# Strassen products moved from the MLP's up-projection to its down-projection, more low parts made by transfers, one shared transpose for two norms

## The chip, the cores and the metric

The kernel runs on one core of a Trainium2 chip. The core has five engines with a queue of instructions each: PE (TensorE, the matrix unit; its weight loads are shown apart as PEld), DVE (VectorE), ACT (ScalarE), POOL (GpSimd) and SP (SyncE, which here only issues transfers); 16 DMA engines move data between the device's memory and the on-chip SBUF. Matrix products are accumulated in eight PSUM banks. An engine works through its queue in order and waits there for what others have to finish. The metric is the device time of one execution in microseconds (us).

## The reference

The input is one sequence of 512 tokens with 1,024 features, in float32. Layer A attends to keys that a small indexer selects, layer B attends with a forget-gate bias to keys and values computed once from the stream. Each layer ends with the same MLP:

```python
def sq_relu_mlp(xn, w_up, w_down):
    return jnp.square(jax.nn.relu(xn @ w_up)) @ w_down

def reference(...):
    h = x
    for layer in range(DEPTH):
        if layer < N_A:
            h = h + dsa_attention(rms_norm(h, g_attn_a[layer]), w_in_a[layer], w_o_a[layer])
        else:
            if layer == N_A:
                k_sh, v_sh, cum_sh = shared_kv(h, g_kv, w_kv_b, b_f)
            j = layer - N_A
            h = h + fox_attention(rms_norm(h, g_attn_b[j]), w_q_b[j], w_o_b[j], k_sh, v_sh, cum_sh)
        h = h + sq_relu_mlp(rms_norm(h, g_mlp[layer]), w_up[layer], w_down[layer])
    return rms_norm(h, g_final)
```

`w_up` is 1024 x 4096, `w_down` 4096 x 1024. At the start of layer B the stream `h` is normalized twice, with two gains (`g_kv`, `g_attn_b`) and the same root mean square.

## The kernel before

Every float32 product is made of three matmuls (`mm3`): each operand is split into a high part, rounded to the type fp32r, and a low part, the rest; high x high, high x low and low x high are summed in a PSUM bank. The high part is a copy on ACT. The low part comes in one of two ways (`wunit`): a subtraction on DVE, or, where `lo_eng` is POOL, ACT writes the negated high part and a transfer issued by POOL adds the raw weights onto it (tile pair `arena_r<-arena` in the trace, 512 KB each). Before, 20 weight blocks of layer A's attention take the second way; all other blocks take the first.

The MLP (`mlp`) works in four quarters of 1,024 hidden features each. In a quarter the up-projection makes the hidden features, transposed (features on partitions, 512 tokens along the row), ReLU and square follow, and the down-projection (`tokprod`) adds 512 output columns at a time onto the stream `h`: per quarter 192 matmuls of 128x512, named `tp`. In the up-projection, `pair` takes two blocks of 128 features and computes them by Winograd's form of Strassen's scheme: the weights (2 x 2 blocks: inner half by feature block) and the tokens (inner half by token half) are added and subtracted on DVE, seven products instead of eight are made (`prod`, 12 matmuls of 128x256 each, named `st`), and DVE adds the results together. The first four feature blocks of a layer are made plainly (`up`). The weight sums are formed anew for each pair, the token sums (`tokside`) once per layer.

The engines' orders are not those of the code. `Recorder` records all operations; `schedule` then simulates them with its own costs, gives each a due time that follows PE's order, and lets each engine take the ready operation that is due first and finds a buffer; `emit` writes the result out. What it assumes for a matmul, for a transfer and for buffers so decides who stands in front of whom. Buffers are cut from two arenas in SBUF, one for float32 (54 KB a partition) and one for fp32r (144 KB), in any size.

At the end of layer A's MLP, `afterA` is called for each block of 128 tokens: root mean square, product with the gain `g_attn_b`, eight transposes on PE (`yT`), splitting; the same is then repeated with `g_kv` for the keys and values of layer B: 64 transposes in all for the two norms.

## Time and profile before

| | |
|---|---|
| time, median of 3 runs | 1193.82 us (1193.72 to 1194.06) |
| profiled execution: own time | 1194.9 us |
| profiled execution: span in the trace | 1193.1 us |
| PE busy | 1171.7 us, 98% |
| DVE busy | 867.2 us, 73% |
| ACT busy | 656.5 us, 55% |
| POOL busy | 166.0 us, 14% |
| moved by DMA | 126.14 MB, mean 106 GB/s |

Busy time is the union of an engine's instructions, so 98% says that PE has hardly a gap, not that each matmul runs at its best. All operations are emitted from one source line (L454), so that groups are told apart by the names of their tiles: `tp`, `st`, `up`, `qp`, `kp`, `lg`, `pv` and so on are PSUM banks.

### The profile page before, as it was taken

Reading aid. Unit: us, or ns where it says so; the run is one execution under the profiler, and the core shown is the slowest. Engines: PE = TensorE matmul, PEld = TensorE weight load, DVE = VectorE, ACT = ScalarE, POOL = GpSimd, SP = SyncE. Lnnn points to the kernel's source line nnn. Section 1 sums busy time; section 2 is a strip of 40 time slices with the busy share of each in tenths; the row PEclk is TensorE's granted clock in tenths of the full one; section 3 lists DMA queues with packets and bytes.
Section 4 is the critical chain, followed back from the end, with each engine's and each line's share of the span. In section 5 each row is a group of like instructions: output and inputs, shape, how many; then the busy total and the mean of one; then the engine's idle time right before and its main releaser. Section 6 shows DMA issues by size and latency. Waiting matters only on the chain.

```text
span 1193.1 us, 18921 instructions
## 1 busy us (share of the span) xinstructions
PE 1171.7 (98%) x6932; PEld 1027.7 (86%) x6932; DVE 867.2 (73%) x1774; ACT 656.5 (55%) x1309; POOL 166.0 (14%) x303
## 2 busy tenths in 40 slices
PE   8999899999999999999999999999999999999997
PEld 7878677899899899898897888778998998998986
DVE  6799978778486576676766559987785874866753
ACT  7831789748345355364434069985583453452632
POOL 0401444100000000000000077772000000000010
PEclk8999899999999999999999999999999999999999
DMA  9920065616224224425440202543152242242301
GB/s 326 205 54 1 3 192 141 177 39 189 78 68 154 77 70 124 124 69 163 158 126 18 72 24 79 179 127 107 36 181 85 74 139 89 72 141 72 124 2 71
DMA packets 95519, 126.14 MB, mean 106 GB/s; under 512 B 6193, under 2 KB 61489, under 8 KB 95426
## 3 DMA queue, kind: packets, MB, share of 16 engines
q1 hardware_dynamic: 92546, 114.45, 30.1%
q0 software_dynamic: 2880, 10.49, 4.6%
q8 instruction: 55, 0.90, 0.3%
q14 instruction: 38, 0.31, 0.1%
HBM read 110.20 MB, written 4.23 MB: 96 GB/s over the span
## 4 chain that ended last, share of the span: by engine, by line
PE 91%; DVE 3%; ACT 2%; DMA 2%; issue 1%; POOL 0%; SPq 0%; DVEq 0%; POOLq 0%; ACTq 0%
PE tp L454 46%; PE st L454 23%; PE up L454 4%; PE qp L454 4%; PE pv L454 3%; PE lg L454 3%; PE kp L454 3%; PE pT L454 3%; ACT arena_r L454 1%; DVE arena_r L454 1%; PE yT L454 1%; DVE arena L454 1%; ACT arena L454 1%; DMA arena<-in_w_in_a_dram 1%; DMA arena_r<-arena 1%
## 5 line engine op out<-in xcount | busy, mean ns | idle before, releaser
L454 PE MATMUL tp<-arena_r 128*128 128x512 f32 (+3 forms) x2592 | 596.1, 385 | 2.4 <-DMA arena_r<-arena 1.5
L454 PEld LDWEIGHTS tp<-arena_r 128*128 128x128 f32 x2592 | 473.0, 189 | 93.0 <-DMA arena_r<-arena 1.8
L454 DVE TENSOR_TENSOR arena_r<-arena,arena_r 128x512 fp32r<-128x512 f32 (+4 forms) x396 | 321.9, 835 | 153.4 <-PE tp L454 90.1
L454 ACT CAST arena_r<-arena 128x512 fp32r<-128x512 f32 (+5 forms) x416 | 299.5, 752 | 242.8 <-PE tp L454 150.3
L454 PEld LDWEIGHTS st<-arena_r 128*128 128x128 f32 x2352 | 283.4, 192 | 0.6
L454 PE MATMUL st<-arena_r 128*128 128x256 f32 x2352 | 283.8, 283 | 0.0
L454 ACT ACTIVATE arena<-arena 128x512 f32<-128x512 f32 (+1 forms) x162 | 100.6, 627 | 84.3 <-DVE arena L454 77.1
L454 POOL TENSOR_SCALAR arena<-arena,cq 128x128 f32<-128x128 f32 (+3 forms) x64 | 36.4, 583 | 484.7 <-ACT cq L454 475.9
L454 DVE TENSOR_TENSOR arena<-arena 128x512 f32<-128x512 f32 (+4 forms) x145 | 99.3, 699 | 2.6 <-ACT arena L454 1.3
L454 DVE TENSOR_TENSOR arena<-tp,arena 128x512 f32<-128x512 f32 (+1 forms) x81 | 54.9, 683 | 51.0 <-PE tp L454 49.7
L454 DVE TENSOR_TENSOR arena<-st,arena 128x256 f32<-128x256 f32 x196 | 77.0, 418 | 17.5 <-PE st L454 13.8
L454 POOL TENSOR_SCALAR arena<-arena,rc 128x128 f32<-128x128 f32 (+3 forms) x128 | 75.6, 610 | 65.6 <-DVE rc L454 63.2
L454 ACT ACTIVATE arena<-arena,mn 128x384 f32<-128x384 f32 (+3 forms) x128 | 71.4, 562 | 21.6 <-issue 18.1
L454 POOL TENSOR_TENSOR arena<-arena 128x512 f32<-128x512 f32 (+2 forms) x18 | 20.4, 1149 | 411.0 <-DVE arena L454 410.7
L454 DVE CUSTOM_DVE_ANT_0 arena<-lg,arena 128x128 f32<-128x128 f32 (+3 forms) x128 | 58.8, 484 | 10.0 <-PE pT L454 3.1
L454 PE MATMUL lg<-arena_r 128*128 128x128 f32 (+3 forms) x256 | 64.2, 348 | 0.1
L454 PE MATMUL kp<-arena_r 128*128 128x512 f32 x192 | 54.5, 402 | 1.2 <-DVE arena_r L454 1.2
L454 PE MATMUL pT<-ident,arena 128*128 128x128 f32 x320 | 53.2, 281 | 1.8 <-DVE arena_r L454 0.9
L454 PEld LDWEIGHTS pT<-ident,arena 128*128 128x128 f32 x320 | 39.6, 143 | 12.8 <-POOL arena L454 4.7
L454 PEld LDWEIGHTS lg<-arena_r 128*128 128x128 f32 x256 | 43.7, 199 | 6.0 <-issue 1.5
L454 PE MATMUL up<-arena_r 128*128 128x256 f32 x384 | 47.5, 284 | 0.0
L454 PE MATMUL qp<-arena_r 128*128 128x256 f32 (+1 forms) x288 | 47.0, 321 | 0.0
(91 smaller groups left out, 913.6 us busy)
## 6 DMA issues: line engine op xcount, KB each, us to landing
arena<-in_w_up_dram SPq DMA_DIRECT2D x64, 512.0 KB, 4.0
arena<-in_w_down_dram SPq DMA_DIRECT2D x64, 512.0 KB, 3.6
arena_r<-arena POOLq DMA_DIRECT2D x20, 512.0 KB, 6.8
arena<-in_w_kv_b_dram SPq DMA_DIRECT2D x16, 512.0 KB, 4.8
arena<-in_w_in_a_dram SPq DMA_DIRECT2D x12, 512.0 KB, 6.3
arena<-in_x_dram SPq DMA_DIRECT2D x8, 512.0 KB, 6.2
arena<-in_w_o_a_dram SPq DMA_DIRECT2D x8, 512.0 KB, 6.1
arena<-in_w_q_b_dram SPq DMA_DIRECT2D x8, 512.0 KB, 5.1
```

The source lines that it names most:

```text
L454: getattr(self.engs[o.eng], o.fn)(*a, **k)
```

## The change

- The up-projection is computed plainly: per feature block 24 matmuls of 128x512 (for the first four blocks of a layer 48 of 128x256, as before).
- The down-projection takes Strassen's scheme in Winograd's form: 2 x 2 blocks of the hidden activations (token half by half of the quarter's features, tile `sq`) and of the weights (half of the features by half of the output columns). Per quarter there are seven products of 24 matmuls of 128x512 (`tp<-dhi,xhi`). Sums of the weights are made on DVE in place (`raw<-raw`), those of the activations too; results go to `h` and, for the part that two quadrants share, to two tiles `share`. Two pairs of banks are used twice: the second product is accumulated onto the first after DVE (or ACT, in the first quarter) has read the first. Two of the four weight quarters are loaded twice, so that 96 blocks of 512 KB of `w_down` are loaded instead of 64.
- Low parts by transfers ("dl") now also for the up-projections, layer B's queries, values and output projection: 108 blocks instead of 20. Those of the down-projection and of layer B's keys stay on DVE.
- The schedule's costs: 13.3 ns on top of each matmul's columns instead of 3, later landings for POOL's transfers; new limits ("ahead") on how early a weight buffer may be taken. Buffers are now slots of fixed size: 41 of 4 KB, 18 of 2 KB, 7 of 1 KB, 8 of 512 bytes, one of 256 bytes.
- Layer B's two norms share one scaled row tile and 32 transposes; the two gains are applied per feature while the result is split. The gains are loaded as columns of eight values per partition.
- In the last norm the halves change roles for the last token blocks, since the left half of the columns is now the last to be finished.

```diff
+                c = (2.0 if o.eng != "POOL" else 5.0) + o.cost if o.fn == "dma_start" else o.cost + self.LAT.get((o.eng, s.eng), 0.1)
...
+                        if x[2].seq - low >= t.pool.reach or x[2].prio - pec > t.pool.ahead:
...
+    "ahead": {"wr": 40, "wh": 30, "wl": 30},
+    "slots": {1024: 41, 512: 18, 256: 7, 128: 8, 64: 1}, "sizes": (8, 8, 8, 8), "sq": 'S', "x8": 400, "h": 200, "wr": 1500,
...
+    def lows(stage):
+        lo_eng[0] = G if stage in CFG["dl"] else V
...
-        def pair(c0, done):
-            raw = [rec.tile(p_wr, [128, 4, 256], F32, "raw") for _ in range(2)]
...
-            a11 = wop(A[0, 0])
-            a12 = wop(A[0, 1])
...
-            o4 = wop(wsum(A[0, 1], s2, OP.subtract))
-            o3 = wop(wsum(A[0, 0], A[1, 0], OP.subtract))
-            a22 = wop(A[1, 1])
...
-            S.copy(k1, prod(a11, B[0, 0]))
-            add(r1[:, lo], prod(a12, B[1, 0]), k1)
-            add(u2, prod(o2, tm["t2"]), k1)
-            add(z, prod(o1, tm["t1"]), u2)
-            add(r1[:, hi], prod(o4, B[1, 1]), z)
-            S.activation(r1, r1, AF.Relu)
...
-            for f in range(f, nf, 2):
-                pair(f0 + 128 * f, lambda i, r, f=f: relu_done(f + i, r))
...
-            tokprod(hl, wd, f0, nf, 0, 512, addto(0), order="t" if lastc else "k")
...
+        lows("up1" if last else "up0")
...
+        share = [htile([128, 512], "share") for _ in range(2)]
+        def xop(src):
+            out = []
+            for k in range(0, 4, 2):
+                hl = tuple(rec.tile(p_x8, [128, 2, H], F32R, n) for n in ("xhi", "xlo"))
+                split(hl[0], hl[1], src[:, k:k + 2, :])
+                out.append(hl)
+            return out
         def wop(src):
+            out = []
+            for y in src:
+                hl = rec.tile(p_wh, [128, 2, 512], F32R, "dhi"), rec.tile(p_wl, [128, 2, 512], F32R, "dlo")
+                split(hl[0], hl[1], y)
+                out.append(hl)
+            return out
...
+        def part(b, x, w, start, i, c=slice(0, 512), js=range(2)):
+            for j in js:
+                for k in (2 * j, 2 * j + 1):
+                    mm3(b[:, c], tuple(u[:, k % 2, 128 * i:128 * i + 128] for u in x[j]),
+                        tuple(u[:, k % 2, c] for u in w[j]), start and k == 0, k == 3, skip_group_check=True)
+        def prod(bs, x, w, start, whole=False):
+            if whole:
+                for i in range(2):
+                    part(bs[i], x, w, start, i)
+            else:
+                for j in range(2):
+                    for i in range(2):
+                        part(bs[i], x, w, start, i, js=(j,))
...
+            X = {(i, j): rec.tile(p_x8, [128, 4, H], F32, "sq") for i in range(2) for j in range(2)}
+            f0 = 1024 * ci
+            def relu_done(f, b):
+                r = scr([128, T], "r")
+                S.activation(r, b, AF.Relu)
+                for i in range(2):
+                    S.activation(X[i, f // 4][:, f % 4, :], r[:, tl[i]], AF.Square)
...
+            for f in range(f, 8):
+                b = bank([128, T], "up")
+                featprod(xT, wS(wu, f0 + 128 * f), b)
+                relu_done(f, b)
+            def raw(j, n):
+                ys = []
+                for k in range(f0 + 512 * j, f0 + 512 * j + 512, 256):
+                    ys.append(rec.tile(p_wr, [128, 2, 512], F32, "raw"))
+                    SP.dma_start(ys[-1], wd[k:k + 256, 512 * n:512 * n + 512].rearrange("(k p) c -> p k c", p=128))
+                return ys
+            lastc = ci == 3
+            def addh(i, half, src, c=slice(0, 512)):
+                o = h[i][:, 512 * half + c.start:512 * half + c.stop]
+                add(o, src[:, c], o)
+            y11 = raw(0, 0)
+            w11 = wop(y11)
+            a = banks()
+            prod(a, xop(X[0, 0]), w11, True)
+            for i in range(2):
+                if ci:
+                    add(share[i], a[i], share[i])
+                else:
+                    S.copy(share[i], a[i])
+            prod(a, xop(X[0, 1]), wop(raw(1, 0)), False)
+            for i in range(2):
+                addh(i, 0, a[i])
+            s1 = rec.tile(p_s4, [128, 4, H], F32, "s1")
+            V.tensor_tensor(s1, X[1, 0], X[1, 1], op=OP.add)
+            sub(y11, raw(0, 1), y11)
+            b = banks()
+            prod(b, xop(s1), wop(y11), True)
+            for i in range(2):
+                addh(2 + i, 1, b[i])
+            V.tensor_tensor(X[1, 0], X[0, 0], X[1, 0], op=OP.subtract)
+            V.tensor_tensor(s1, s1, X[0, 0], op=OP.subtract)
+            V.tensor_tensor(X[0, 1], X[0, 1], s1, op=OP.subtract)
+            y22 = raw(1, 1)
+            sub(y11, y22, y11)
+            d = banks()
+            prod(d, xop(s1), wop(y11), True)
+            for i in range(2):
+                add(share[i], d[i], share[i])
+                if lastc:
+                    addh(i, 1, share[i])
+            prod(b, xop(X[0, 1]), wop(y22), False, lastc)
+            for i in range(2):
+                addh(i, 1, b[i])
+                if lastc:
+                    after(i)
+            y12 = raw(0, 1)
+            sub(y12, y22, y12)
+            c = banks()
+            prod(c, xop(X[1, 0]), wop(y12), True)
+            for i in range(2):
+                addh(2 + i, 1, c[i])
+                if lastc:
+                    addh(2 + i, 1, share[i])
+                    addh(2 + i, 0, share[i])
+            x22 = xop(X[1, 1])
+            y21 = raw(1, 0)
+            sub(y21, y21, y11)
+            w4 = wop(y21)
+            if not lastc:
+                prod(c, x22, w4, False)
+                for i in range(2):
+                    addh(2 + i, 0, c[i])
+            else:
+                for i in range(2):
+                    for q in ((0, 512),) if not last or i == 0 else ((0, 256), (256, 512)):
+                        q = slice(*q)
+                        part(c[i], x22, w4, False, i, q)
+                        addh(2 + i, 0, c[i], q)
+                    after(2 + i)
...
-    for t in range(NT):
-        norm_T(h[t], gk[t], g, state["kv"], t)
...
+    xq, xk = new_xT(), new_xT()
+        ys[t] = [scr([128, 512], "y") for _ in range(2)]
+        for i in range(2):
+            V.tensor_scalar(ys[t][i], h[t][:, 512 * i:512 * i + 512], r, None, op0=OP.mult)
         SP.dma_start(hd[128 * t:128 * t + 128], h[t])
-    xq, xk = state["q"], state["kv"]
+        if t % 2:
+            c = slice(128 * t - 128, 128 * t + 128)
+            for k in range(0, 8, 2):
+                b = bank([128, 2, 256], "yT")
+                for i in range(2):
+                    for u in range(2):
+                        o = 128 * ((k + i) % 4)
+                        PE.transpose(b[:, i, 128 * u:128 * u + 128], ys[t - 1 + u][k // 4][:, o:o + 128], ident)
+                for x, g in ((xq, gq), (xk, gkv)):
+                    for i in range(2):
+                        split(x[0][k // 2][:, i, c], x[1][k // 2][:, i, c], b[:, i, :], scale=g[:, k + i:k + i + 1])
...
+        cuts = (0, 256, 512, D) if t == NT - 1 else (0, 512, D)```

How the queues change is seen at three places. The first is PE's queue in layer A's MLP. Before (numbers left out of the names), quarters of up-projection (`st`) and of down-projection (`tp`) follow each other in blocks:

```order
L454 MATMUL up<-arena_r 128x256 x146
L454 MATMUL st<-arena_r 128x256 x168
L454 MATMUL tp<-arena_r 128x512 x192
L454 MATMUL st<-arena_r 128x256 x336
L454 MATMUL tp<-arena_r 128x512 x192
```

Now, with the buffers' numbers, the place in the second quarter at which the first product (in banks `tp_4124` and `tp_4137`, weights `dhi_3901`) ends and the second one (weights `dhi_3935` and `dhi_3948`) is accumulated onto it:

```order
L416 MATMUL tp_4137<-dhi_3901,xhi_3985 128x512
L416 MATMUL tp_4137<-dlo_3923,xhi_3985 128x512
L416 MATMUL tp_4137<-dhi_3901,xlo_3994 128x512
L416 MATMUL tp_4124<-dhi_3935,xhi_4067 128x512
L416 MATMUL tp_4124<-dlo_3943,xhi_4067 128x512
L416 MATMUL tp_4124<-dhi_3935,xlo_4074 128x512
L416 MATMUL tp_4124<-dhi_3935,xhi_4067 128x512
L416 MATMUL tp_4124<-dlo_3943,xhi_4067 128x512
L416 MATMUL tp_4124<-dhi_3935,xlo_4074 128x512
L416 MATMUL tp_4124<-dhi_3948,xhi_4144 128x512
L416 MATMUL tp_4137<-dhi_3935,xhi_4067 128x512
```

Seven matmuls into the other bank stand between the end of the first product in `tp_4137` and its continuation. The `st` matmuls are gone from the queue.

The second place is DVE's queue at that point. Before, in the corresponding up-projection, the additions out of PSUM (`arena<-st`) stand between splits and sums of weights:

```order
L454 TENSOR_TENSOR arena<-st,arena 128x256
L454 TENSOR_TENSOR arena_r<-arena,arena_r 128x1024
L454 TENSOR_TENSOR arena<-st,arena 128x256 x3
L454 TENSOR_TENSOR arena<-arena 128x512 x3
L454 TENSOR_TENSOR arena<-st,arena 128x256
L454 TENSOR_TENSOR arena_r<-arena,arena_r 128x512 x4
```

Now (`s1` and `sq` are sums of activations, `xlo` low parts of activations, `share` the shared result):

```order
L416 TENSOR_TENSOR s1_4148<-sq_3857,sq_4030 128x1024
L416 TENSOR_TENSOR xlo_4159<-sq_4027,xhi_4144 128x512
L416 TENSOR_TENSOR share_3534<-tp_4124,share_3534 128x512
L416 TENSOR_TENSOR xlo_4171<-s1_4148,xhi_4162 128x512
L416 TENSOR_TENSOR xlo_4178<-s1_4148,xhi_4167 128x512
L416 TENSOR_TENSOR share_3555<-tp_4137,share_3555 128x512
L416 TENSOR_TENSOR s1_4148<-s1_4148,sq_3854 128x1024
L416 TENSOR_TENSOR sq_3857<-sq_3854,sq_3857 128x1024
```

The two reads of the banks stand behind one sum and three low parts of activations.

The third place is ACT's queue at the end of that quarter. Before, there stand casts of raw weights and results of `st`:

```order
L454 CAST arena_r<-arena 128x1024
L454 ACTIVATE arena<-arena 128x512
L454 COPY arena<-st 128x256
L454 ACTIVATE arena<-arena 128x512
L454 CAST arena_r<-arena 128x1024
```

Now the last five of the next quarter's eight up-weight blocks (`whi` the high part, `wlo` the negated one, onto which POOL's transfer adds) and the first ReLU of that quarter:

```order
L416 CAST whi_4332<-raw_4230 128x1024
L416 ACTIVATE wlo_4340<-whi_4324 128x1024
L416 ACTIVATE wlo_4349<-whi_4332 128x1024
L416 CAST whi_4364<-raw_4256 128x1024
L416 ACTIVATE wlo_4373<-whi_4364 128x1024
L416 CAST whi_4399<-raw_4292 128x1024
L416 ACTIVATE wlo_4407<-whi_4399 128x1024
L416 CAST whi_4430<-raw_4344 128x1024
L416 ACTIVATE wlo_4440<-whi_4430 128x1024
L416 ACTIVATE r_4480<-up_4445 128x512
```

All eight blocks are prepared in front of the quarter's first ReLU. On POOL's queue 52 transfers now stand in a row, from layer A's output projection to layer B's values, where two stood before.

## Rows read from the trace of the kernel before

**Rows 1.** The head of the profile's page: the span, the busy time of each engine, and the granted clock of PE in 40 slices (tenths of 2.4 GHz).

```profile
span 1193.1 us, 18921 instructions
...
PE 1171.7 (98%) x6932; PEld 1027.7 (86%) x6932; DVE 867.2 (73%) x1774; ACT 656.5 (55%) x1309; POOL 166.0 (14%) x303
...
PEclk8999899999999999999999999999999999999999
```

**Rows 2.** The chain that ended last: shares of the span by engine and by line and tile.

```profile
PE 91%; DVE 3%; ACT 2%; DMA 2%; issue 1%; POOL 0%; SPq 0%; DVEq 0%; POOLq 0%; ACTq 0%
PE tp L454 46%; PE st L454 23%; PE up L454 4%; PE qp L454 4%; PE pv L454 3%; PE lg L454 3%; PE kp L454 3%; PE pT L454 3%; ACT arena_r L454 1%; DVE arena_r L454 1%; PE yT L454 1%; DVE arena L454 1%; ACT arena L454 1%; DMA arena<-in_w_in_a_dram 1%; DMA arena_r<-arena 1%
```

**Rows 3.** Stretches of the span: from and to, length, then busy time (and number of instructions) of PE, PEld, DVE, ACT and POOL, the granted clock of PE (1.00 is 2.4 GHz), the DMA engines' busy share and GB/s. The rows are the start, two places of layer A's attention, the first MLP, the step to layer B, a place of layer B's attention, and the end.

```profile
0.00:21.00 21.00, 15.63 (x69) 12.60 (x69) 11.30 (x39) 13.42 (x40) 0.70 (x6) 0.76 0.96 314
...
120.00:140.00 20.00, 16.59 (x86) 13.18 (x85) 18.55 (x69) 13.16 (x44) 9.39 (x16) 0.83 0.00 1
...
160.00:180.00 20.00, 17.92 (x91) 14.04 (x90) 12.75 (x39) 16.33 (x37) 8.77 (x15) 0.91 0.56 149
...
273.00:504.00 231.00, 231.00 (x1415) 208.51 (x1414) 157.31 (x260) 111.41 (x184) 0.00 (x0) 1.00 0.34 107
...
548.00:606.00 58.00, 56.99 (x313) 48.19 (x312) 40.02 (x89) 28.52 (x69) 0.00 (x0) 1.00 0.54 169
...
750.00:780.00 30.00, 29.40 (x159) 22.82 (x157) 28.94 (x63) 28.37 (x64) 21.45 (x36) 1.00 0.51 176
...
1145.00:1193.00 48.00, 41.14 (x204) 34.80 (x202) 18.62 (x47) 14.06 (x36) 5.17 (x4) 0.97 0.12 45
```

**Rows 4.** The chain of waits in order of time: start, length, what (xcount of instructions in a row).

```profile
292.95 43.55 PE tp L454 x192
336.50 40.31 PE st L454 x336
...
577.87 0.44 PE yT L454 x4
```

**Rows 5.** PE's instructions grouped by tile and shape: busy time, mean of one in ns (with the pipeline's latency), idle time before them.

```profile
L454 PE MATMUL tp<-arena_r 128*128 128x512 f32 x2376 | 564.3, 392 | 2.2 <-DMA arena_r<-arena 1.5 <-ACT arena_r L454 0.6
L454 PE MATMUL st<-arena_r 128*128 128x256 f32 x2352 | 283.8, 283 | 0.0
...
L454 PE MATMUL yT<-ident,arena 128*128 128x128 f32 x160 | 25.6, 290 | 4.1 <-DVE arena L454 3.7
...
L454 PE MATMUL qp<-arena_r 128*128 128x512 f32 x96 | 21.9, 389 | 0.0
```

**Rows 6.** DVE's instructions by shape, the same columns.

```profile
L454 DVE TENSOR_TENSOR arena_r<-arena,arena_r 128x512 fp32r<-128x512 f32 x267 | 177.1, 687 | 79.8 <-PE tp L454 50.3 <-ACT arena_r L454 18.7 <-PE st L454 6.2
L454 DVE TENSOR_TENSOR arena_r<-arena,arena_r 128x1024 fp32r<-128x1024 f32 x112 | 136.9, 1228 | 72.7 <-PE tp L454 39.9 <-PE st L454 16.2 <-PE qp L454 10.2
...
L454 DVE TENSOR_TENSOR arena<-tp,arena 128x512 f32<-128x512 f32 x79 | 54.0, 689 | 49.3 <-PE tp L454 48.0
...
L454 DVE TENSOR_TENSOR arena<-arena 128x1024 f32<-128x1024 f32 x8 | 9.8, 1221 | 1.4 <-ACT arena L454 1.3
```

**Rows 7.** ACT's instructions by shape.

```profile
L454 ACT CAST arena_r<-arena 128x512 fp32r<-128x512 f32 x267 | 158.4, 619 | 181.3 <-PE tp L454 138.5 <-DVE arena L454 12.2 <-DMA arena<-in_w_up_dram 11.9
L454 ACT CAST arena_r<-arena 128x1024 fp32r<-128x1024 f32 x132 | 137.0, 1049 | 61.5 <-DMA arena<-in_w_down_dram 13.5 <-PE tp L454 11.9 <-PE qp L454 9.4
...
L454 ACT ACTIVATE arena_r<-arena_r 128x1024 fp32r<-128x1024 f32 x20 | 20.7, 1060 | 1.1 <-PE pv L454 0.6 <-PE tp L454 0.3 <-PE lg L454 0.2
...
L454 ACT ACTIVATE arena<-up 128x512 f32<-128x512 f32 x8 | 4.6, 595 | 0.7 <-DVE arena_r L454 0.4 <-DVE arena L454 0.2
...
L454 ACT CAST arena_r<-arena 128x256 fp32r<-128x256 f32 x8 | 3.2, 402 | 0.1
```

**Rows 8.** The DMA queues (packets, MB, share of the 16 engines' span; q1 are SP's transfers, q0 POOL's) and transfers by line (count, KB each, median us from issue to landing).

```profile
q1 hardware_dynamic: 92546, 114.45, 30.1%
q0 software_dynamic: 2880, 10.49, 4.6%
...
arena<-in_w_up_dram SPq DMA_DIRECT2D x64, 512.0 KB, 4.0
...
arena_r<-arena POOLq DMA_DIRECT2D x20, 512.0 KB, 6.8
```

**Rows 9.** POOL's adding transfers: the time POOL needs to issue one (min/median/max ns), and from issue to landing (us).

```profile
L454 POOL DMA_DIRECT2D arena_r<-arena x20: 826/862/1205, 24.6 to 216.0; - x20
...
DMA to landing us min/median/max: 4.5/6.8/13.0
```

**Rows 10.** Two stretches near the start, in which loads and adding transfers run together; columns as in rows 3.

```profile
30.00:40.00 10.00, 10.00 (x78) 9.86 (x77) 5.08 (x17) 8.12 (x16) 6.16 (x8) 1.00 1.06 256
40.00:50.00 10.00, 9.94 (x61) 8.34 (x59) 9.14 (x30) 9.52 (x16) 4.51 (x7) 1.00 1.03 219
```

**Rows 11.** The chain of waits at the end, in order of time: the last matmuls, and the first step behind them.

```profile
1144.72 40.84 PE tp L454 x200
...
1185.59 0.44 DVE arena L454
```

More of the change, by code (lines that the diff above doesn't have):

```diff
@@ L118, in give @@
         self.slots.append(at)
[L121 to L152 removed]
 class Op:
[L156 removed]
+    __slots__ = ("eng", "fn", "a", "k", "prio", "preds", "succ", "n", "cost", "tiles", "new", "end", "ready", "lock", "seq", "clk")
 class Recorder:
@@ L280, in schedule @@
             o.prio = clock
+            o.clk = clock
             if o.eng == "PE":
@@ L303, in schedule @@
             if u.max() > r.cap:
-                raise RuntimeError("%s needs %d at %d" % (getattr(r, "tag", "arena"), u.max(), u.argmax()))
-        now, cnt, low, lock = 0.0, 0, 0, 0.0
+                raise RuntimeError("%s needs %d at %d" % (r.tag, u.max(), u.argmax()))
+        now, cnt, low, lock, pec = 0.0, 0, 0, 0.0, 0.0
         def release(o):
@@ L392, in schedule @@
                     dma[0] = st + o.cost
-                    o.end = dma[0] + 1.0
+                    o.end = dma[0] + (1.0 if e != "POOL" else 2.5)
                 else:
@@ L429, in schedule @@
                          for e, a in avail.items() if a]
-                gaps = {t.arena.tile.dtype if 0 else len(t.arena.gaps): t.arena.gaps for t in self.all if t.arena}
-                raise RuntimeError("schedule is stuck at %.1f: %d %s %s" % (now, low, gaps, stuck))
+                raise RuntimeError("schedule is stuck at %.1f: %d %s" % (now, low, stuck))
             now = min(nxt)
@@ L1032, in body @@
+    ys = {}
+    mlp(xT, a["w_up"][0], a["w_down"][0], afterA)
     qo = [big([128, 2, T], "qo") for _ in range(8)]
@@ L1102, in body @@
     S.copy(cq, cb)
[L1104 removed]
+    lows("k")
     def kproj(p):
```

242 lines of the change are left out of this document (69 added, 173 removed), and 1 row of the table CFG.

## The prediction

> **What bounds the kernel now.** I read the page's head first, then the chain that ended last, then stretches of the span, then the groups by shape. PE is busy for 1171.7 of 1193.1 us and its clock is granted in full nearly everywhere [rows 1]; 91% of the chain is PE, 46% of it `tp` and 23% `st` [rows 2]. In the first MLP PE is busy for 231.00 of 231.00 us, DVE for 157, ACT for 111, and the DMA engines a third of the time [rows 3]. So in the MLPs the time is the sum of PE's matmuls, and everything else has slack. PE's idle time is 21.4 us in all, and most of it is not in the MLPs: 5.4 at the start, 3.4 and 2.1 in two places of layer A's attention, 1.0 at the step to layer B, 0.6 in layer B's attention, 6.9 at the end [rows 3].
>
> How fast PE runs, busy time does not say; the unbroken streams of the chain do: 192 matmuls of 128x512 take 43.55 us, 226.8 ns each, and 336 of 128x256 take 40.31 us, 120.0 ns each [rows 4]. Two short ones cost 240.0 ns, 13.2 more than one long one with as many columns.
>
> **The matmuls of the MLPs.** Of the short `st` there are 2352 [rows 5]; they go: 2352 x 0.1200 = 282.2 us. In their place the plain up-projection has 28 blocks a layer, 24 matmuls each, 1344 in both layers. The down-projection had 2 x 4 x 192 = 1536 long ones and gets 2 x 4 x 7 x 24 = 1344. That is 1152 more long ones: 1152 x 0.2268 = 261.3 us. The difference is -20.9 us. In columns it is only 12,288 of 0.6 million fewer (5 us); the rest is the shorter list of instructions. Bounds: with the group's mean for `tp`, 564.3/2376 = 237.5 ns, which holds stretches mixed with other work, it is 282.2 - 273.6 = -8.6; with the group's 283.8 us for `st`, -22.5 [rows 5]. I take the stream, since the new products run as streams too, and the group `qp` with the same operands as the new up-projection shows 21.9/96 = 228 ns [rows 5].
>
> A rule speaks against this term: the Trainium skill, "TensorE: Matmul & The Clock Gate", section "Back-to-back issue gap", gives an isolated matmul N/2.4 + 2.5 ns, thus 109.2 for 256 columns and 215.8 for 512; by it the term would be an estimated 256.8 - 248.6, only -8.2 us. The trace disagrees at both lengths, with 120.0 and 226.8.
>
> **The transposes.** 32 of 64 go. Four in a row take 0.44 us on the chain [rows 4], so -3.5 us; by the group's mean, 25.6/160 = 0.16 each [rows 5], -5.1. I take -3.5, as that place is PE-bound but for 1.0 us [rows 3]. The casts and subtractions for two normalized copies stay.
>
> **What the Strassen sums cost.** Work of DVE per quarter, with the shapes' means [rows 6]: 14 weight low parts at 1.228, 8 weight sums and 4 activation sums at 1.221, 14 activation low parts at 0.687, 14 additions out of PSUM at 0.689: 17.2 + 14.7 + 9.6 + 9.6 = 51.1 us. ACT [rows 7]: 22 casts at 1.049, 8 negations at 1.060, 8 ReLUs at 0.595, 16 squares of 256 at 0.402, 14 casts at 0.619: 51.4 us. A quarter's matmuls take 192 + 168 = 360 x 0.2268 = 81.7 us. Both engines are at 63%, so I cost these edits at nothing; their cover is the up stage of 43.5 us, in which DVE has only weights to prepare. Without it the 51 us would not fit beside the down stage's 38.1.
>
> Where the cover is thin is the change of products in the same banks. After the last up-matmul, ReLU and two squares end at about 1.5 us; DVE then does the sum (to 3.0) and a low part (3.7), reads the first bank, done at 4.1, until 4.8, does two low parts (6.1) and reads the second, until 6.8. PE ends the first product at 24 x 0.2268 = 5.44 and has seven matmuls more before it needs that bank: 7.03. It fits by 0.2 us. There are 14 such handovers behind DVE. Bounds: below, nothing, as in the MLP before PE never idled though DVE read the banks at each product [rows 3]; above, one 1.228 us instruction in front of each, 17.2 us [rows 6]. I take +1.5, near the lower end.
>
> **The low parts by transfer.** 88 more. A 512 KB load occupies all 16 engines for 30.1% x 1193.1 / 114.45 MB x 0.524 = 1.65 us, an adding transfer for 4.6% x 1193.1 / 20 = 2.74 us [rows 8]. Per quarter 20 loads and 8 adding transfers are 54.9 of 81.7 us, 67%; before it was 34%. Landing takes 4.5 to 13.0 us [rows 9]; the long ones come where the engines are full [rows 10]. ACT prepares all eight blocks of the next quarter in front of its first ReLU, by the walk above from some 12 us into the down stage of 38.1 on, and POOL has nothing else there to stand behind; the first is needed 26 us later. I cost it at nothing; without that lead see the first rival.
>
> The Trainium skill ("SBUF — State Buffer", "SBUF: two separate sides") warns that POOL cannot write a transfer's descriptors while DVE runs a two-port instruction. Here POOL took 826 to 1205 ns per issue [rows 9] with DVE busy for 9.14 of 10 us in one of those stretches [rows 10], so a third of a microsecond at worst; the lead covers it, and the sum is the same by either.
>
> **The attentions.** Their PE work is the same, but buffers are now slots, and the queues changed: before the last attention product 38 instead of 65 matmuls of the output projection fill gaps in layer A, 35 instead of 70 in layer B. Fewer fillers are either fewer gaps or more idle time: from -2.7 us (the idle 2.1 and 0.6 gone) to 62 x 0.2268 = +14.1. DVE, at 28.94 of 30 us in layer B's attention [rows 3], is relieved of 8 x 1.228 = 9.8 us, while ACT, at 28.37, gets 8 x 1.060 more. I take +2, nearer to the small end.
>
> Start and end stay: the end is a chain from the last matmul (1185.6) on [rows 11], with the same steps on the other half; the two gain columns are small loads where layer A's start keeps the queues full [rows 10], inside the attentions' bounds.
>
> **Sum.** 1193.1 - 20.9 - 3.5 + 1.5 + 2.0 = 1172.2 us of span. The profiled execution took 1194.9, 1.8 more than its span: 1174.0. It lies 1.1 above the median of the runs, so I predict 1173.
>
> **Rivals.**
> - *The up-weights land late.* SP loads twelve blocks of `w_down` before seven of a next quarter's eight up-blocks; if slots free late, the prepared lead is gone, and at each of six quarter starts PE waits for load, cast, negation, issue and landing: 4.0 + 1.05 + 1.06 + 0.86 + 6.8 = 13.8 us [rows 7 to 9]. All of it is +83; half, +41: 1214. It decides for slower from 23/6 = 3.9 us per quarter on. For it: the DMA share doubles. Against it: ACT's queue as shown. 7%.
> - *Handovers.* Each waits for one long DVE instruction: 1173 - 1.5 + 17.2 = 1189. For it: 0.2 us of slack. Against: most long ones stand elsewhere. 10%.
> - *Attentions starve on slots:* 1173 - 2 + 14 = 1185. 12%.
> - *Better:* transposes at -5.1, no handover waits, less idle in the attentions: 1173 - 1.6 - 1.6 - 1.5 - 4.7 = about 1164. 8%.
> - *The new long matmuls run at their group's mean* of 237.5 ns instead of the stream's, because more of their operands come late: -8.6 instead of -20.9, 1173 + 12.3 = 1185. For it: the mean is a row; against it: the stream of rows 4 is the same work. 2%. The page's gaps above would come out close to it.
>
> **How the numbers follow.** The forecast has 61%, its own range 1166 to 1181. Runs of this kernel tell 0.2% (2.4 us) from no change: below 1191.4 is faster, above 1196.2 slower. Faster: 61 + 8 + 2, and 8 of the handovers' 10 and 10 of the attentions' 12: 89%. Same: 2 and 1, 3%. Slower: 7 and 1, 8%. The range 1163 to 1188 leaves out the late weights, the worst handovers and a little below.
>
> **What would show it.** In the changed profile: streams of 192 up-matmuls in 43.5 us and 168 down-matmuls in 38.1 us with PE's clock full; PE idle in the MLPs under 2 us; its busy sum near 1147; yT at 128; DVE and ACT near 63% in the MLPs, the DMA engines near 67%. PE waiting in the MLPs on a transfer would show the first rival, on DVE the second, more than 5.5 us idle in the attentions the third; long matmuls well over 227 ns would break the main term.

## The result and the profile after

The changed kernel takes 1180.76 us (median of 4 runs, 1180.23 to 1181.78), the kernel before, run beside it, 1193.77: a ratio of 0.9892, with an interval from 0.9875 to 0.9909. It is 13.0 us faster. Predicted were 1173 and a gain of 20.8. The span of its profiled execution is 1179.7 us, 13.4 shorter than in [rows 1].

The head of the page of after, and its two large DMA queues (packets, MB, share of the 16 engines' span):

```profile
span 1179.7 us, 16374 instructions
...
PE 1154.7 (98%) x5688; PEld 959.0 (81%) x5688; DVE 773.3 (66%) x1474; ACT 737.5 (63%) x1385; POOL 235.4 (20%) x391
...
PEclk9999799999999999999999999999999999999999
...
q1 hardware_dynamic: 131714, 130.18, 35.1%
q0 software_dynamic: 15552, 56.63, 24.8%
```

PE is as full as before (98%) with 1,244 instructions fewer; ACT has grown from 55% to 63%, POOL's transfers from 4.6% to 24.8% of the DMA engines [rows 1, 8]. One slice of the clock, at about 130 us, shows 7.

The first MLP, over the same stretch as in [rows 3], and the unbroken streams of two quarters in the chain of waits, to hold against [rows 4]:

```profile
273.00:504.00 231.00, 231.00 (x1034) 191.21 (x1033) 137.75 (x157) 134.90 (x196) 20.09 (x23) 1.00 0.66 175
```

```profile
925.10 43.07 PE up L416 x190
968.16 37.80 PE tp L416 x166
1006.87 43.07 PE up L416 x190
1049.94 37.80 PE tp L416 x166
```

Long matmuls take 226.7 and 227.7 ns each, and from one up stream to the next are 81.8 us (forecast 81.7). (At the change back to the up-projection the two kinds alternate, and the chain lists those few apart.) PE never idles there.

So that kernels can be compared, I cut each span at four instructions: layer A's first attention scores (`lg`), its first up-matmul, the `fb` product behind the shared norm and the queries, and layer B's first up-matmul. Columns as in [rows 3]. The kernel before:

```profile
0.00:121.82 121.82, 116.21 (x604) 98.60 (x605) 105.17 (x296) 65.07 (x137) 22.72 (x32) 0.96 0.54 143
121.82:248.64 126.82, 121.31 (x629) 95.79 (x628) 100.94 (x286) 104.81 (x255) 43.66 (x76) 0.96 0.46 121
248.64:642.20 393.56, 392.55 (x2499) 356.77 (x2498) 273.87 (x466) 194.98 (x339) 0.00 (x0) 1.00 0.35 109
642.20:846.35 204.15, 201.85 (x1038) 166.14 (x1036) 156.16 (x337) 128.62 (x301) 94.48 (x192) 1.00 0.28 89
846.35:1193.00 346.65, 339.79 (x2171) 310.42 (x2169) 231.10 (x393) 163.01 (x280) 5.17 (x4) 1.00 0.29 93
```

And after:

```profile
0.00:126.36 126.36, 120.22 (x608) 99.93 (x609) 109.46 (x300) 65.31 (x137) 22.02 (x31) 0.99 0.66 180
126.36:252.56 126.20, 121.23 (x626) 95.63 (x625) 90.40 (x276) 107.84 (x258) 50.30 (x82) 0.95 0.43 99
252.56:632.40 379.84, 379.29 (x1868) 320.19 (x1867) 228.68 (x313) 236.14 (x376) 35.27 (x40) 1.00 0.70 185
632.40:839.40 207.00, 202.81 (x1029) 166.07 (x1028) 135.77 (x319) 139.60 (x313) 98.82 (x208) 0.99 0.51 131
839.40:1179.70 340.30, 331.18 (x1565) 277.22 (x1563) 208.99 (x269) 188.66 (x304) 28.96 (x31) 0.99 0.59 162
```

Stage by stage the change is +4.5, -0.6, -13.7, +2.9 and -6.4 us. The third stage, one MLP with the transposes, was forecast at -13.2 (half of -20.9, all of -3.5, half of +1.5). The others together were forecast at -7.7 and came to +0.4. A table at the end of the experiments gives the same five stages for every kernel.

### The profile page after: what moved, and what is told of

Read it like the earlier page. It is cut to its first block, busy times and chain, and to the rows that moved or that the text cites. A ratio compares the mean times of both kernels' runs of the same rounds, so it can differ in the third digit from the quotient of the medians.

```text
span 1179.7 us, 16374 instructions
## 1 busy us (share of the span) xinstructions
PE 1154.7 (98%) x5688; PEld 959.0 (81%) x5688; DVE 773.3 (66%) x1474; ACT 737.5 (63%) x1385; POOL 235.4 (20%) x391
## 3 DMA queue, kind: packets, MB, share of 16 engines
q1 hardware_dynamic: 131714, 130.18, 35.1%
q0 software_dynamic: 15552, 56.63, 24.8%
## 5 line engine op out<-in xcount | busy, mean ns | idle before, releaser
L416 PE MATMUL up<-xT,whi 128*128 128x512 f32 (+1 forms) x1152 | 323.4, 366 | 0.0
L416 PEld LDWEIGHTS up<-xT,whi 128*128 128x128 f32 x1152 | 207.9, 189 | 34.8
L416 POOL DMA_DIRECT2D wlo<-raw x108 | 95.3, 883 | 702.1 <-ACT wlo L416 291.7
L416 DVE TENSOR_TENSOR dlo<-raw,dhi 128x1024 fp32r<-128x1024 f32 x112 | 136.3, 1226 | 143.4 <-ACT dhi L416 89.3
L416 PE MATMUL up<-xT,wlo 128*128 128x512 f32 (+1 forms) x576 | 210.0, 366 | 0.0
L416 PE MATMUL tp<-dhi,xhi 128*128 128x512 f32 (+1 forms) x452 | 171.8, 389 | 1.2 <-DVE h L416 0.8
L416 PE MATMUL tp<-dlo,xhi 128*128 128x512 f32 (+1 forms) x452 | 171.5, 387 | 0.0
L416 PE MATMUL tp<-dhi,xlo 128*128 128x512 f32 (+1 forms) x452 | 170.8, 388 | 0.0
L416 ACT CAST whi<-raw 128x1024 fp32r<-128x1024 f32 (+2 forms) x124 | 124.2, 1025 | 74.2 <-DMA raw<-in_w_up_dram 66.3
L416 ACT CAST dhi<-raw 128x1024 fp32r<-128x1024 f32 x112 | 116.5, 1047 | 66.3 <-PE up L416 64.1
L416 ACT ACTIVATE wlo<-whi 128x1024 fp32r<-128x1024 f32 x108 | 112.7, 1061 | 23.9 <-DMA wlo<-raw 10.6
L416 PE MATMUL tp<-whi,xT 128*128 128x512 f32 (+2 forms) x432 | 123.5, 372 | 0.0
L416 PEld LDWEIGHTS up<-xT,wlo 128*128 128x128 f32 x576 | 108.4, 189 | 17.5
L416 DVE TENSOR_TENSOR h<-tp,h 128x512 f32<-128x512 f32 (+1 forms) x97 | 64.6, 681 | 80.8 <-PE tp L416 80.7
L416 PEld LDWEIGHTS tp<-dhi,xhi 128*128 128x128 f32 x452 | 84.8, 188 | 21.5 <-DVE h L416 1.4
L416 PEld LDWEIGHTS tp<-dhi,xlo 128*128 128x128 f32 x452 | 84.7, 188 | 17.4
L416 PEld LDWEIGHTS tp<-dlo,xhi 128*128 128x128 f32 x452 | 84.9, 188 | 16.9
L416 DVE TENSOR_TENSOR raw<-raw 128x1024 f32<-128x1024 f32 x64 | 76.6, 1220 | 19.3 <-DMA raw<-in_w_down_dram 18.7
L416 PEld LDWEIGHTS tp<-whi,xT 128*128 128x128 f32 x432 | 78.8, 192 | 12.2 <-ACT xT L416 0.2
L416 ACT ACTIVATE r<-up 128x512 f32<-128x512 f32 x64 | 37.9, 592 | 79.6 <-PE up L416 79.6
L416 ACT ACTIVATE l<-l,mn 128x128 f32<-128x128 f32 (+3 forms) x128 | 71.5, 563 | 22.4 <-DVE mn L416 22.0
L416 POOL TENSOR_SCALAR l<-l,rc 128x128 f32<-128x128 f32 (+3 forms) x128 | 69.1, 561 | 59.4 <-DVE rc L416 42.5
## 6 DMA issues: line engine op xcount, KB each, us to landing
wlo<-raw POOLq DMA_DIRECT2D x108, 512.0 KB, 8.6
raw<-in_w_down_dram SPq DMA_DIRECT2D x96, 512.0 KB, 11.5
raw<-in_w_up_dram SPq DMA_DIRECT2D x64, 512.0 KB, 6.7
raw<-in_w_kv_b_dram SPq DMA_DIRECT2D x16, 512.0 KB, 5.6
raw<-in_w_in_a_dram SPq DMA_DIRECT2D x12, 512.0 KB, 6.5
raw<-in_w_o_a_dram SPq DMA_DIRECT2D x8, 512.0 KB, 4.8
raw<-in_w_q_b_dram SPq DMA_DIRECT2D x8, 512.0 KB, 7.2
```

What stands on the lines that cost most here:

```text
L416: getattr(self.engs[o.eng], o.fn)(*a, **k)
```

## The experiments

All kernels compute the whole reference. Medians in us; the kernel before, run beside them, took 1192.3 to 1194.2.

**Late gain columns.**

```diff
-        g = const([128, 8], name)
+        g = rec.tile(VPool(rcst, name, 1, ahead=60), [128, 8], F32, name)
```

> The kernel after with one thing changed: the loads of the two gain columns gq and gkv (1,024 elements of 4 bytes each, issued by SP at 16.2 and 16.7 us) may be issued only 60 us ahead of their use by the planner's clock, so that SP loads the last w_in_a blocks without a break. All other queues keep their order. Theory: in the kernel after, the traffic falls from some 380 to 40 GB/s for two microseconds behind these loads (24 to 26 us), the weights behind them land late, ACT waits 3.0 us at 31 to 34, and DVE's first MAX8 of the top-k search, the chain of layer A's attention, starts at 46.4 us instead of 43.6 in the kernel before. Then the first MAX8 comes 2 to 3 us earlier, first up-matmul at 249 to 251 instead of 252.6, and the time is 1180.8 - 2.8 = about 1178. Rival: the late start comes from the new order and the slots (POOL's rope additions that hold DVE's k for 2.5 us at 31); then MAX8 stays at 46 and the time at 1180 to 1181.5.

1181.13, ratio 0.9895 [0.9882, 0.9909]: no gain. The first MAX8 came at 45.56 us instead of 46.39. But in two kernels below whose queues begin as in after (`plain_down`, `short_up`) it came at 45.42 and 47.49, so 0.8 is within what this start repeats to. The traffic does fall behind the 4-byte loads (to 5 GB/s from 22 to 23 us, earlier than the text above has it; 391 in this run), but the time does not hang on it. The time is the rival's.

**Output weights of layer B back on DVE**, and **all but layer A's input weights back on DVE** (up-projections, queries, values and both output weights). Layer A's eight output blocks, which the kernel before makes by transfer, are among them, so that 96 blocks change and 12 adding transfers are left; the expectation below counts 88.

```diff
-"dl": ("a", "oa", "up0", "up1", "q", "v", "ob")
+"dl": ("a", "oa", "up0", "up1", "q", "v")
```

```diff
-"dl": ("a", "oa", "up0", "up1", "q", "v", "ob")
+"dl": ("a",)
```

> The kernel after with the low parts of layer B's output weights (8 blocks of 512 KB) subtracted by DVE again, instead of negated by ACT and added by a transfer. Theory: ACT is busy for 9.9 of 10 us from 740 to 790 in the kernel after and sets the pace of layer B's attention there; 8 x 1.06 = 8.5 us go from it, 8 x 1.23 = 9.8 come to DVE (about 65% busy in layer B's attention). The stretch from the last fb matmul to the first up-matmul of layer B, 207.0 us, falls to 204 to 206, the time to 1178 to 1180. Rival: buffers and order hold the attention back; then the time stays within 1 us of 1180.8, or rises by up to 3 where DVE becomes the late one.

> The kernel after with the low parts of all stages but layer A's input and attention weights made by DVE again (output weights of both layers, up-projections, queries, values): 88 adding transfers and 88 ACT negations of 1.06 us go, 88 subtractions of 1.23 us come to DVE. Theory: a quarter has 81.7 us of matmuls, DVE 51.1 - hidden - and gets 9.8 more, ACT loses 8.5; the MLPs keep their time, the attention of layer B gains what no_ob gains: 1178 to 1181. Rival: the transfers are what keeps DVE free for the handovers of the banks; with the subtractions back in its queue, the 14 handovers and the last quarter wait up to 1.23 us each: up to 1181 + 17 = 1198, 1186 if a third does.

1182.26 (0.9905 [0.9891, 0.9918]) and 1184.82 (0.9923 [0.991, 0.9935]). The first theory falls: with the output weights of layer B back on DVE (`no_ob`) ACT, though it had been full, was not what held layer B's attention; the stage became 1.0 longer. The second run shows where the transfers work. Its stages from the second to the last:

```profile
126.31:255.33 129.02, 122.77 (x619) 94.41 (x617) 105.74 (x289) 94.20 (x242) 41.91 (x68) 0.95 0.15 42
255.33:635.10 379.77, 379.31 (x1873) 320.99 (x1872) 275.36 (x356) 197.78 (x335) 0.00 (x0) 1.00 0.43 128
635.10:843.12 208.02, 203.29 (x1029) 165.40 (x1028) 152.51 (x335) 126.19 (x297) 92.96 (x192) 1.00 0.31 94
843.12:1183.40 340.28, 331.12 (x1565) 277.13 (x1563) 236.77 (x294) 164.59 (x278) 5.88 (x4) 0.99 0.39 119
```

Both MLP stages keep their length to 0.1 us, with POOL all but idle and DVE at 275 instead of 229 us in the first: there the transfers neither cost nor bring anything. Beside the attentions they bring 2.8 and 1.0 us; the 2.8, in layer A, are not the change's alone, since they include layer A's output blocks.

**Long up-matmuls cut in two.**

```diff
-                featprod(xT, wS(wu, f0 + 128 * f), b)
+                u = wS(wu, f0 + 128 * f)
+                for half in range(2):
+                    featprod(xT, u, b, tl[half])
```

> The kernel after with each of the 56 x 24 = 1,344 up-matmuls of 512 columns cut into two of 256 (same banks, same weights, same columns in all; the 8 blocks that were halved before stay so). Theory: rows 4 price, 120.0 ns for 256 columns and 226.8 for 512: 1344 x (240.0 - 226.8) = +17.7 us, 1198.5, and streams of 384 matmuls in about 46.1 us. Rival, the Trainium skill's gap of 2.5 ns per matmul (TensorE: Matmul & The Clock Gate, Back-to-back issue gap): 1344 x 2.6 = +3.5 us, 1184. If short and long cost the same per column, 1181.

1199.85, ratio 1.0049 [1.0034, 1.0065], 19.1 over after. The chain has its up streams as

```profile
936.41 45.72 PE up L416 x381
```

that is 120.0 ns each, as in [rows 4]. The two MLP stages grew by 9.2 and 9.7 us for 672 pairs each, 13.7 and 14.4 ns per pair (forecast 13.2). The price of a short instruction is shown. The gap of the Trainium skill (TensorE: Matmul & The Clock Gate, Back-to-back issue gap), which the page gives for an isolated matmul, would have made +3.5: these streams do not follow it.

**Rope additions of one tile on DVE.**

```diff
-            G.tensor_tensor(dst, dst, tmp, op=OP.add)
+            eng.tensor_tensor(dst, dst, tmp, op=OP.add)
...
+            rope(q[:, 0:192].heads(64), b[:, 0:192].heads(64), t, 3, eng=V if t == 1 else G)
...
+        rope(q[:, 0:320].heads(64), b[:, 0:320].heads(64), t, 5, eng=V if t == 1 else G)
```

> The kernel after with the two rope additions of token tile 1 in layer A's index projection (192 and 320 elements a row) on DVE instead of POOL; else the queues differ in a few rows. Theory: in the kernel after, DVE's sum k needs 2.50 us instead of 0.29, from 31.15 to 33.65, because POOL's two additions run at that time; PE waits 1.6 us for its transposed copy (kb), the scores follow, and the first MAX8 is late. On DVE the additions take some 0.25 + 0.40 us: MAX8 at 46.4 - 2.2 + 0.7 = 44.9, the time 1180.8 - 1.5 = 1179.3. Rival: the weights and the transfers behind them (ACT waits 3.0 us at 31) set the start; then k is short, but MAX8 stays at 46 or later, and the time within 0.7 of 1180.8.

1180.07, ratio 0.9886 [0.9871, 0.9902]: 0.7 less, about what two medians differ by. In the profile `k` takes 0.43 us, the first MAX8 is at 44.63, the first scores 1.75 earlier. The theory is right on the place; in the time the rival's bound (within 0.7 of 1180.8) holds as well, so that a gain is not shown. The rows of after that show the block, DVE's and POOL's in order of time:

```profile
31.15 2.50 DVE L416 TENSOR_TENSOR k<-qr,rtmp 128x128 f32<-128x128 f32 x1
```

```profile
30.87 0.89 POOL L416 TENSOR_TENSOR qr<-qr,rtmp 128x192 f32<-128x192 f32 x1
31.41 1.18 POOL L416 DMA_DIRECT2D wlo<-raw  x1
32.03 1.45 POOL L416 TENSOR_TENSOR qi<-qi,rtmp 128x320 f32<-128x320 f32 x1
```

DVE's sum of 128 columns, else 0.28 us, ends only as POOL's second addition does. The Trainium skill (SBUF — State Buffer, Who interferes with whom) says that a DVE instruction with two SBUF inputs contends with a POOL instruction that reads SBUF; the rows agree.

**The planner's new numbers alone, in the kernel before.**

```diff
-            return n / 2400.0 + 0.003
+            return max(n / 2400.0 + 0.0133, 0.109)
...
-                o.end = dma[0] + 1.0
+                o.end = dma[0] + (1.0 if e != "POOL" else 2.5)
```

(and the due time and factor of an adding transfer, as in the change).

> The kernel before with the four changed numbers of the planner (matmul, adding transfer twice, landing of POOL's transfers) and nothing else. Theory: the 6.9 us that layer A up to its first up-matmul (+4.0) and the stretch from fb to layer B's first up-matmul (+2.9) cost in the kernel after come from the order that these numbers make: about 1200. Rival: they come from the slots, the limits on early loads and the transfers; then 1193.8 within 2 us, and first up-matmul near 248.6.

1212.22, ratio 1.0154 [1.0141, 1.0168]: 18 us slower with the same instructions in another order, more than the theory had. +3.8 up to the first scores and +4.9 in layer B's attention lie where after had lost, too; but layer A's attention has +2.7, and the MLP stages have +3.2 and +2.1.

**The shared transposes alone, in the kernel before** (the diff is that part of the change).

> The kernel before with only the shared norm transposes of layer B (32 transposes instead of 64, gains as columns, applied when the banks are read). Theory: 32 x 0.11 = -3.5 us, 1190.3 (-5.1 by the group's mean, 1188.7). Rival: the transposes of a pair of tiles now wait for two normalized tiles, and the scaled copies for ACT and DVE; half of the gain goes: 1192.

1191.8, ratio 0.998 [0.9972, 0.9989]: -2.4. In their own stage they gave 4.8 us (388.73 instead of 393.56), more than forecast; the newly made plan of layer B's attention, with the same 1,038 matmuls, gave 2.2 back in idle time.

**Plain down-projection in after** (Strassen sums out, `tokprod` as in before).

```diff
-            y11 = raw(0, 0)
-            w11 = wop(y11)
...
+            tokprod(hl, wd, f0, 8, 0, 512, addto(0), order="t" if lastc else "k")
```

> The kernel after with both MLPs' down-projection as plain products: 8 quarters x 24 = 192 matmuls of 512 columns more, no Strassen sums. What the Strassen products are worth by themselves, their sums and handovers included. Theory (the sums are hidden, PE sets the MLPs): +192 x 0.2268 = +43.5, 1224.3. Rival: the handovers and the last quarter, where the down stage took 38.7 and 40.4 us instead of 38.1, are what was lost: 7 x 0.6 + 2.3 = 6.5 less, 1217.8.

1221.38, ratio 1.023 [1.0216, 1.0244]: +40.6, between the two. The MLP stages grew by 19.8 and 20.1 instead of 21.8 each: sums and handovers cost 3.7 us in all in this order, 1.5 were forecast. The Strassen products are worth 41 us here.

**The planner's old numbers in after**, all four, and then **the old price of a matmul alone**:

```diff
-            return max(n / 2400.0 + 0.0133, 0.109)
+            return n / 2400.0 + 0.003
```

> The kernel after with the planner's old numbers (matmul n/2400 + 0.003, adding transfer twice, POOL's transfers landing as any other); products, transposes, transfers and slots stay those of after. Theory: the new numbers cost the orders around the attentions 4 to 7 us, as they cost the kernel before 18: then layer A up to its first up-matmul falls from 252.6 to about 249 and the stretch fb to up from 207.0 to 204, with MLP A at 379.8: 1174 to 1177. Rival: each set of numbers belongs to the kernel that was planned with it; with the old ones the plan lets the adding transfers start late (it takes them to land 1.5 us earlier), and the time is 1185 or more, the loss again outside the MLP streams or at their starts.

> The kernel after with only the planner's price of a matmul put back (n/2400 + 0.003 us instead of at least 0.109 and n/2400 + 0.0133); its numbers for the transfers stay new. It tells which of the numbers cost the 12.2 us between after and oldcost. Theory: the price of a matmul, since PE's clock in the plan sets every instruction's due time and the plan of PE differs most here (3,752 rows from after, 914 from oldcost): two thirds of 12.2 or more come back, 1168.5 to 1172.5, with 7 us of it before layer A's first up-matmul. Rival: the transfers' numbers (due 5.0 instead of 2.0 us ahead, landing 1.5 later), which put the preparation of weights ahead of the attentions' own work: then 1178 to 1182 here.

1168.58 (0.9791 [0.9774, 0.9807]) and 1164.55 (0.9766 [0.9751, 0.978]). With the old numbers the change is worth 25 us instead of 13, and the price of a matmul alone costs 16.2 by the medians (15.0 by the ratios to the kernel before run beside each). `oldmm`, with the new numbers for the transfers, is 4.0 (3.0) faster than `oldcost`. The first theory had the cause and half its size; the rival, that old numbers suit only the old kernel, falls. The stages with the old price of a matmul:

```profile
0.00:121.81 121.81, 117.90 (x604) 99.75 (x605) 103.77 (x292) 65.23 (x137) 22.52 (x32) 0.99 0.70 191
121.81:244.79 122.98, 119.06 (x626) 94.78 (x624) 93.64 (x283) 106.66 (x258) 49.99 (x82) 0.97 0.43 97
244.79:623.00 378.21, 378.12 (x1871) 320.99 (x1870) 230.15 (x314) 236.34 (x376) 35.50 (x41) 1.00 0.72 187
623.00:823.75 200.75, 200.26 (x1030) 165.51 (x1028) 136.18 (x319) 140.25 (x313) 99.70 (x208) 1.00 0.51 133
823.75:1162.40 338.65, 330.11 (x1565) 277.54 (x1563) 211.24 (x269) 188.74 (x304) 29.38 (x31) 0.99 0.60 163
```

The same instructions as in after; each stage is shorter, the first and the fourth most (4.6 and 6.3).

**Three small edits together**: late gain columns, rope additions on DVE, and the last token tile's last two products in two banks.

```diff
+                c.append(bank([128, 512], "tp"))
+                qs2 = ((0, slice(0, 512), 0), (1, slice(0, 256), 1), (1, slice(256, 512), 2))
```

> The kernel after with three edits: the rope additions of k_first, the late gain columns of gain_late, and, in layer B's last quarter, the last two products of token tile 3 accumulated in two banks (columns 0 to 255 and 256 to 511) instead of one, so that the second half need not wait until DVE has read the first. Theory: in the kernel after PE waits 0.83 us for DVE's read at 1170.2; without it the stage from the first up-matmul of layer B to the end takes 340.3 - 0.8 + 0.2 (12 more short matmuls) = 339.7; with first lg at 124.6 as in k_first the time is 1180.8 - 0.7 - 0.6 = 1179.5 or less. Rival: the end is DVE's and ACT's chain behind the last matmul (7.8 us), which waits for the same readings; then the stage stays at 340.3 and the time at 1180.

1179.5, ratio 0.9882 [0.9867, 0.9897], as forecast. The last stage takes 339.73 instead of 340.30; the wait for DVE's read of the bank fell from 0.8 to 0.4 us.

**The price of a matmul one step lower still**, with the two banks.

```diff
-            return n / 2400.0 + 0.003
+            return n / 2400.0 - 0.0073
```

> The kernel oldmm with the planner's price of a matmul one equal step lower (n/2400 - 0.0073 us; after has + 0.0133, oldmm + 0.003, a step of 0.0103), and the two banks for the last products of combo. It tells whether the 16.2 us between after and oldmm are a rule (PE priced under what it takes makes the plan bring the other engines' work earlier) or one plan among many. Theory, a rule: PE idle in the attentions stays at oldmm's level, layer A up to its first up-matmul within 2 us of 244.8, fb to up within 2 of 200.8, the time 1160 to 1166. Rival, chance of a plan: the MLP stages stay (378 and 338 us less 0.6 for the two banks), but the attentions scatter by several us, to 1168 or more.

1167.6, ratio 0.9773 [0.9759, 0.9786], between theory and rival. The fourth stage stays short (199.89), as the theory has it; the first is 5.3 longer than in `oldmm`, by one wait of PE of 4.9 us for DVE's `kr` at 75 us. So there is no rule "the lower, the better", but both low prices give better plans than 13.3 ns did. Nor is it the luck of one plan: the six kernels with these products and the new price (after, `gain_late`, `no_ob`, `lows_dve`, `k_first`, `combo`) took 1179.5 to 1184.8, the three with a low price 1164.6 to 1168.6.

Lengths of the five stages (to the first `lg`; to the first up-matmul; to `fb`; to layer B's first up-matmul; to the end), worked out from the same kind of rows:

| kernel | 1 | 2 | 3 | 4 | 5 | span |
|---|---|---|---|---|---|---|
| before | 121.8 | 126.8 | 393.6 | 204.2 | 346.7 | 1193.1 |
| before_newcost | 125.7 | 129.6 | 396.8 | 209.1 | 348.7 | 1209.8 |
| before_shared | 121.1 | 126.4 | 388.7 | 206.4 | 347.7 | 1190.2 |
| after | 126.4 | 126.2 | 379.8 | 207.0 | 340.3 | 1179.7 |
| gain_late | 125.5 | 125.8 | 379.8 | 207.0 | 340.3 | 1178.4 |
| no_ob | 126.4 | 126.2 | 379.7 | 208.0 | 340.2 | 1180.5 |
| k_first | 124.6 | 126.4 | 379.8 | 205.9 | 340.2 | 1176.9 |
| lows_dve | 126.3 | 129.0 | 379.8 | 208.0 | 340.3 | 1183.4 |
| plain_down | 125.4 | 126.7 | 399.6 | 207.3 | 360.4 | 1219.4 |
| short_up | 127.5 | 126.5 | 389.0 | 206.4 | 350.0 | 1199.4 |
| combo | 125.1 | 125.6 | 379.8 | 207.3 | 339.7 | 1177.5 |
| oldcost | 122.8 | 122.7 | 378.4 | 204.0 | 339.0 | 1166.9 |
| oldmm | 121.8 | 123.0 | 378.2 | 200.8 | 338.7 | 1162.4 |
| lowmm | 127.1 | 122.2 | 379.0 | 199.9 | 338.1 | 1166.3 |

## Why the prediction was right and where it failed

The direction and the main term were right. *The matmuls of the MLPs*, -20.9: the streams run at the forecast 227 ns, `short_up` confirms 120.0 ns for a short one, and DVE (60%), ACT (58%) and the DMA engines (66%) hide the Strassen work in the first MLP as said. *The transposes*, -3.5, gave 4.8 in their stage. *The handovers*, +1.5, were mis-sized: 3.7 by `plain_down`. (Three of the four pairs of banks are used twice, not two as the text ahead has it; in the third another product stands between the two, so the count of 14 stays.) Part of the 3.7 is layer B's last quarter: there the sums and low parts stand in front of `xhi` on DVE and ACT, and PE waits 0.4 us, and 0.8 more for DVE's read of a bank in front of the last half product:

```profile
PE tp L416 <- DVE h L416: 0.8, 1, 0.8
PE tp L416 <- ACT xhi L416: 0.4, 1, 0.4
```

With the old price of a matmul the two MLP stages are 1.6 and 1.7 us shorter, with the same products; so most of the 3.7 seems to come with the order, too. A plain down-projection at that price was not run.

*The low parts by transfer at nothing* was right, and more so than I meant: in the MLPs they also bring nothing.

The step that failed is *The attentions*, +2.0: they cost 7.7. Layer A up to the MLP cost +3.9; layer B's stage +2.9, and some 0.9 more, since eight transposes of the next norm (0.11 us each [rows 4]) no longer stand in it, but behind layer B's first up-matmul. That is 5.7 of the 7.5 us by which the span missed its sum; the rest lies in the MLP stages. I had bounded this term by the idle rows of before (-2.7) and by fewer fillers (+14.1), and put the fillers down to the slots. It was the planner's price of a matmul, which I read in the diff and gave no term of its own. Without that edit (`oldmm`) the same stages come out at -3.9 for layer A and -3.4 for layer B's attention (-2.5 with the transposes counted in), below my lower bound, and the kernel at 1164.55, 8 under the forecast. Two of the signs that I had named show it: PE's busy sum is 1154.7 us, not near 1147 (1145.4 in `oldmm`), and in the stages of the two attentions PE idles for 9.2 us (7.8 before, 4.4 in `oldmm`). So a loss that I had not priced and a gain in the attentions that I had not expected partly cancelled; that the sum came as near as 8 us is in part luck. Of that gain `no_ob` and `lows_dve` each give 1.0 to transfers of layer B (measured around after); the rest was not taken apart. In the kernel before only the four numbers together were tried, not the price alone. The rival *attentions starve on slots* named the place and half its size, but the wrong cause: slots, transfers and quotas are the same in `oldmm`. The rivals of late up-weights and of waiting handovers did not happen: in the first MLP PE is busy for all of 231.00 us.

What the price does, the waits of PE for POOL's results show in part. Before; before with the new numbers; after; and after with the old price:

```profile
PE qT L454 <- POOL arena L454: 1.6, 3, 0.8
...
PE pT L454 <- POOL arena L454: 0.7, 2, 0.5
```

```profile
PE pT L454 <- POOL arena L454: 5.2, 7, 1.3
PE qT L454 <- POOL arena L454: 3.5, 5, 1.8
```

```profile
PE qT L416 <- POOL qr L416: 3.3, 5, 1.0
PE pT L416 <- POOL l L416: 3.1, 3, 2.0
...
PE qT L416 <- POOL qi L416: 0.7, 2, 0.4
```

```profile
PE qT L416 <- POOL qr L416: 0.7, 2, 0.5
...
PE pT L416 <- POOL l L416: 0.2, 1, 0.2
```

That is 2.3 us before, 8.7 and 7.1 with the new price, 0.9 with the old (2.0 in `oldcost`, 1.1 in `lowmm`). Of after's 7.1, 3.9 lie in the second stage and 2.2 in the fourth. In PE's queue 20, 18, 17 and 22 matmuls stand between a group's last scores and its first transposes `pT` for the first four groups of layer A with the new price, and 26, 22, 16 and 25 in `oldmm`. That fits: a matmul that the plan takes to be longer covers a POOL result with fewer of them, and POOL is slower on the chip than in the plan (`l` of 512 columns takes 0.77 us in after, 0.67 in the plan). That this is the mechanism is argued from these rows; no run changed the distance alone, and for `qT` it was not counted. That the price causes the loss is shown by `oldmm`.

These waits are not the whole loss. From layer A's first scores on, after takes 12.8 us more than `oldmm`: in 5.8 of them PE idles, in 7.0 it is busy for longer with the same matmuls, and no run takes these apart. Up to the first scores PE waits for POOL for 1.0 us only. From DVE's first MAX8 to the first scores, in after and in `oldmm` (columns as in [rows 3]):

```profile
46.39:126.36 79.97, 78.77 (x365) 63.17 (x364) 78.92 (x216) 31.11 (x60) 13.18 (x15) 1.00 0.48 126
```

```profile
47.48:121.81 74.33, 73.85 (x346) 60.49 (x345) 73.26 (x200) 29.12 (x58) 13.11 (x15) 1.00 0.52 130
```

PE and DVE are nearly full in both, but in after 19 more matmuls and 16 more DVE instructions, three more MAX8 rounds among them (43 against 40), stand between the two. So the first cut moves with the order, and layer A's two stages are better read together. The first MAX8 itself comes later in `oldmm` (47.48 against 46.39): its lateness is not what the price costs.

It is odd that the new price is the true one: 512/2400 + 0.0133 = 226.6 ns, against 226.8 in [rows 4]. That fits a plan in which other latencies are too short: correcting one of its numbers alone made it worse here.

## What to carry to other kernels

Where a planner writes the order, its numbers are an edit like any other: give them a term of their own, and first run the change with the old numbers and the old kernel with the new ones. Cut the spans at the same instructions and compare stage by stage: stages repeat to 0.1 us where PE is full, and to 2 us at a start or in an attention, so that a loss of a few us can be placed by one run each. Here the truer price of a matmul made the worse order: what is timed is the order, not the cost model.
